# One product with v for both outer key blocks, kept zeros, DVE's other work behind the minimum, and both ends rearranged, in a hybrid attention layer

## The chip, the cores and the metric

The kernel runs on one core of a Trainium2 chip. TensorE (PE) multiplies matrices, VectorE (DVE) and ScalarE (ACT) work on tiles, GpSimd (POOL) does a few tile operations and issues some transfers, SyncE (SP) issues most transfers. The metric is device microseconds of one execution. A separate profiled execution gives the trace; its rows give start and length of each instruction in microseconds.

## The reference, cut to what matters

One layer of an encoder, 512 tokens, width 2048, all float32:

```
h = x @ w_in                                    # (512, 2048) x (2048, 8192)
qa, ka, va, ga, qb, kb, vb, gb = split(h, 1024 columns each)
ya = dilated_attention(qa, ka, va, t5 bias)     # 16 heads of 64, group A
yb = neighbourhood_attention(qb, kb, vb, rpb)   # 16 heads of 64, group B: 8 x 64 grid,
                                                # window of 8 rows x 16 columns
y = concat(ya * silu(ga), yb * silu(gb))
x = layer_norm(alpha * x + y @ w_out) * gain + bias
```

In group B a query sees keys of all 8 rows but of 16 columns only. The kernel cuts the 64 columns into four blocks of 16 queries; the two inner blocks meet 32 key columns each, the two outer ones (0 and 3) 24 each.

## The kernel before, in words

**Products.** Each float32 operand is split in two halves of a shorter format, a high one (ACT copies and rounds it) and a low one (DVE subtracts), by the helper `split` (lines 87 and 88). A product is then three products: high x high, high x low, low x high. Weights come as tiles of 128 x 1024, loaded by SP into a ring of raw tiles, split into a ring of six halves h0 to h5.

**Stages.** `plain_block` (from line 256) makes the gates of the first six head pairs, 16 steps of one tile of x and one of weights; its first weight and x tiles come in slices, so that PE can begin early, and nine products of a zero tile (`WARM`, line 123) run ahead of it. Six `strassen_block`s make k, q and v. From step 0 on, a hand-written order runs the attention: 128 pairs (head h, block b), n = 4h + b, each with `scores(n)`, a minimum over scores plus bias (`softmax`: L520 on DVE; biases have negative sign, so the minimum stands for the maximum), an exponent on ACT (L524), two steps later `turn` (transposes L578 on PE, high copy L583 on ACT, low half L584 on DVE), and in steps with n % 4 = 2 the product with v of the head before (`values`, L596), whose halves are added by L717 (ACT) and L718 (DVE). Between them `fill` puts products of later gates (L459) and of the first half of the output projection (L645). The scores and the product with v share two accumulator banks (`pss`).

**Order.** `later(k, fn)` hands work of ACT and DVE to the close of a step k steps on; `close()` runs it. So the low half of a weight tile (L445), the gate's second part (L465), yk's low half (L630) and copies of partial sums (L651) stand in DVE's order at the end of a step. PE, SP, DVE and ACT keep this written order in the attention; elsewhere a scheduler with a simulated timeline orders each engine, except DVE at the end.

**Group B.** A block's exponent is written to a tile p of two chunks of 128 key positions; the outer blocks fill 192 of 256 columns, and POOL sets the other 64 to zero each time (L567). `near` (line 586) lists the products with v: key chunk, query range, and place in the turned tile; chunk 3 is met by query blocks 0 and 3 in two products of 128 columns.

**End.** The second half of the output projection runs in two parts: column blocks 0 and 1 for all rows, then for each of four row tiles t the column blocks 2 and 3 with weights kept on chip (`wlast`). Then `residual`, `finish` (L765 sum, L766 statistics) and `norm(t)`: aggregate (L782), reciprocal square root (ACT L783, DVE L785), per column block a centring times the gain (L775) and a rescale plus bias (L779), and a transfer out.

Of the kernel before, what the change touches and what calls it, by code (L numbers as in the profile page):

```python
# [6 lines left out]
F32 = mybir.dt.float32  # L7
# [17 lines left out]
WARM = 9  # L25
# [45 lines left out]
def hybrid_layer(tc, xT, xn, w_in, w_early, w_gate, w_out, t5x, brow, rpb, cmask, eye, gain, lbias, out):  # L71
    nc = tc.nc
    from contextlib import ExitStack
    with ExitStack() as ctx:
# [181 lines left out]
        def plain_block(src):  # L256
# [15 lines left out]
            for i in range(8):  # L272
                xr = slot(f"r{i}", F32, "xraw")[:, :1024].rearrange("p (s q) -> p s q", s=2)
                raws.append(xr)
                for s in range(2):
                    k, n = i + 8 * s, 2 * i + s
                    if n == 0:
# [3 lines left out]
                        def xpart(c):  # L281
                            nc.sync.dma_start(xr[:, 0, c], xT[0][:, c])
                            split(xr[:, 0, c], X[0][:, 0, c], X[0][:, 1, c])

                        def wpart(c):
                            nc.sync.dma_start(raw[:, c], src[0][:, c])
                            split(raw[:, c], w[0][:, c], w[1][:, c])
# [142 lines left out]
        def later(k, fn):  # L430

            tasks.setdefault(step[0] + k, []).append(fn)

        def prepare():
# [10 lines left out]
            later(2, lambda: nc.vector.tensor_tensor(l, raw, f(h), ALU.subtract))  # L445
# [7 lines left out]
        def gate_unit(j):  # L453
# [15 lines left out]
            later(1, second)  # L469
# [39 lines left out]
        def softmax(sc, bias, n, grp, i, col, to=0):  # L509

            s = s_ring.next("s")
            p = p_ring.next("p")
# [22 lines left out]

        def load_bias(h):
            g, _, _, hg = head(h)
            bias = ring_b.next("bias")
            n = BW if g else 560
            nc.sync.dma_start(bias[:, :n], bias_d[g][hg])  # L540
            biases[h] = bias

        def scores(n):
# [14 lines left out]
            if g == 0:  # L558
# [3 lines left out]
            at = BIAS[(0, 1, 1, 2)[b]][0]  # L562
            p, exponent = softmax(sc, biases[h][:, at:at + 8 * w].rearrange(rows, r=8), 8 * w, 1, i, 4 * a + b,
                                  64 if b == 0 else 0)
            if w == 24:
                none = 0 if b == 0 else 192
                nc.gpsimd.memset(p[:, none:none + 64], 0.0)  # L567
# [18 lines left out]
        near = ((0, 0, 256, 128), (3, 0, 128, 0), (2, 256, 512, 640), (1, 128, 384, 384), (3, 384, 512, 896))  # L586
        full = tuple((k, 0, 512, 512 * k) for k in range(4))

        def values(h):
# [4 lines left out]
            for m, src in enumerate(turned.pop(h)):  # L594
                for n, (kc, q0, q1, at) in enumerate(parts):
                    nc.tensor.matmul(pv[:, q0:q1], vv[:, kc, a], src[:, at:at + q1 - q0],  # L596
                                     start=m == 0 and n == 0, stop=m == 1 and n == len(parts) - 1)
# [24 lines left out]
        def gated(i):  # L622
# [5 lines left out]
            later(0, lambda: nc.vector.tensor_tensor(y, y, rcs[i], ALU.mult))  # L628
# [275 lines left out]
```

## Time and profile before

| what | value |
| --- | --- |
| timed runs, median (lowest, highest) | 987.69 us (987.32, 988.73) |
| profiled execution, its own time | 987.23 us |
| its span, first to last instruction | 985.4 us |
| PE, DVE, ACT, POOL busy share | 99%, 77%, 50%, 21% |
| mean granted clock of PE | 0.996 |
| stages, by the trace | first products from 4.5 us, first block to about 75, k, q, v to about 560, attention to about 890, output to 975, last normalisation to 985 |

In a row, "x10" counts instructions merged in it, and a bracket tells how long the engine was idle before it and what ended that. A product's length contains its way through the array, so the steps from start to start give the pace.

### The profile page before, as it was taken

What the parts mean: (1) busy time and instruction counts of PE and PEld (TensorE: products, weight loads), DVE (VectorE), ACT (ScalarE), POOL (GpSimd) and SP (SyncE); (2) the same over time, 40 slices, a digit from 0 to 9 for tenths busy, and PEclk for the clock granted to TensorE, in tenths of its full rate; (3) what the DMA queues carried; (4) which work ended last, traced back from release to release, by engine and by line L of the source; (5) the groups of instructions that cost most, each with busy time, mean ns of one, the idle gap of its engine ahead of it and who ended that gap; (6) DMA issues with size and microseconds to landing.
All of it is one profiled execution on the core that took longest, in us unless ns stands there. A gap on an engine that the chain in (4) does not pass through costs nothing.

```text
span 985.4 us, 16207 instructions
## 1 busy us (share of the span) xinstructions
PE 971.5 (99%) x5883; PEld 858.3 (87%) x5883; DVE 756.0 (77%) x1146; ACT 491.6 (50%) x839; POOL 207.6 (21%) x354
## 2 busy tenths in 40 slices
PE   9999999999999999999999999999999999999995
PEld 7889999999888999999888888888888888888885
DVE  7958779678888887877988467676766867777877
ACT  7544444344444344434455365666666676763200
POOL 1003646754754620000000001101110011000021
PEclk9999999999999999999999999999999999999998
DMA  9823697698387558339435967777778788778222
GB/s 345 296 104 70 184 290 251 187 260 234 118 265 250 167 156 274 88 100 270 126 102 171 303 185 208 210 214 234 187 210 232 182 234 207 198 224 294 84 76 96
DMA packets 115888, 194.27 MB, mean 197 GB/s; under 512 B 46351, under 2 KB 65295, under 8 KB 115808
## 3 DMA queue, kind: packets, MB, share of 16 engines
q1 hardware_dynamic: 103552, 169.77, 57.0%
q0 software_dynamic: 12256, 23.47, 8.4%
q8 instruction: 46, 0.75, 0.3%
q14 instruction: 34, 0.28, 0.1%
HBM read 148.67 MB, written 44.50 MB: 196 GB/s over the span
## 4 chain that ended last, share of the span: by engine, by line
PE 95%; DVE 1%; ACT 1%; issue 1%; DMA 1%; POOL 0%; SPq 0%; ACTq 0%; POOLq 0%
PE acc L645 14%; PE acc L459 11%; PE acc L367 11%; PE acc L365 11%; PE acc L366 11%; PE acc L358 5%; PE acc L359 5%; PE acc L360 5%; PE pv L596 4%; PE pt L578 4%; PE acc L267 2%; PE acc L268 2%; PE acc L269 2%; PE sc L556 2%; PE sc L557 2%; PE sc L645 1%
## 5 line engine op out<-in xcount | busy, mean ns | idle before, releaser
L87 ACT ACTIVATE wh<-braw 128x1024 fp32r<-128x1024 f32 x168 | 178.2, 1061 | 239.8 <-PE acc L366 165.2
L88 DVE TENSOR_TENSOR wl<-braw,wh 128x1024 fp32r<-128x1024 f32 x168 | 206.2, 1229 | 74.7 <-ACT wh L87 74.6
L365 PE MATMUL acc<-xk,wh 128*128 128x256 f32 x512 | 143.6, 282 | 1.1 <-ACT wh L87 1.1
L366 PE MATMUL acc<-xk,wh 128*128 128x256 f32 x512 | 143.5, 282 | 0.0
L367 PE MATMUL acc<-xk,wl 128*128 128x256 f32 x512 | 141.1, 282 | 0.0
L373 DVE TENSOR_TENSOR braw<-braw 128x1024 f32<-128x1024 f32 x96 | 117.3, 1235 | 1.1
L645 PE MATMUL acc<-wh,yk 128*128 128x512 f32 x320 | 109.0, 403 | 0.0
L365 PE MATMUL acc<-op,wh 128*128 128x256 f32 x384 | 107.4, 282 | 0.0
L366 PE MATMUL acc<-op,wh 128*128 128x256 f32 x384 | 107.4, 282 | 0.0
L584 DVE TENSOR_TENSOR tl<-pt,th 128x256 fp32r<-128x256 f32 (+1 forms) x128 | 71.1, 555 | 44.8 <-ACT th L583 43.5
L367 PE MATMUL acc<-op,wl 128*128 128x256 f32 x384 | 105.2, 283 | 0.0
L524 ACT ACTIVATE p<-s,mn 128x512 f32<-128x512 f32 (+2 forms) x128 | 76.8, 600 | 51.1 <-DVE mn L520 50.6
L365 PEld LDWEIGHTS acc<-xk,wh 128*128 128x128 f32 x512 | 97.2, 190 | 1.6 <-ACT wh L87 1.5
L366 PEld LDWEIGHTS acc<-xk,wh 128*128 128x128 f32 x512 | 97.2, 190 | 0.1
L367 PEld LDWEIGHTS acc<-xk,wl 128*128 128x128 f32 x512 | 95.8, 190 | 0.0
L583 ACT ACTIVATE th<-pt 128x256 fp32r<-128x256 f32 (+1 forms) x128 | 62.4, 490 | 58.1 <-PE pt L578 55.9
L459 PE MATMUL acc<-xk,wh 128*128 128x512 f32 x320 | 91.0, 403 | 0.0
L520 DVE CUSTOM_DVE_ANT_0 s<-sc,bias 128x512 f32<-128x512 f32 (+2 forms) x128 | 68.0, 531 | 14.6 <-PE sc L557 14.2
L367 PEld LDWEIGHTS acc<-op,wl 128*128 128x128 f32 x384 | 71.5, 190 | 1.7 <-DVE wl L88 1.7
L365 PEld LDWEIGHTS acc<-op,wh 128*128 128x128 f32 x384 | 73.0, 190 | 0.0
L366 PEld LDWEIGHTS acc<-op,wh 128*128 128x128 f32 x384 | 73.0, 190 | 0.0
L645 PEld LDWEIGHTS acc<-wh,yk 128*128 128x128 f32 x320 | 58.5, 189 | 8.9
(157 smaller groups left out, 2036.1 us busy)
## 6 DMA issues: line engine op xcount, KB each, us to landing
braw<-in_w_in SPq DMA_DIRECT2D x96, 512.0 KB
wraw<-in_w_out SPq DMA_DIRECT2D x32, 512.0 KB
wraw<-in_w_gate SPq DMA_DIRECT2D x20, 512.0 KB
k_d<-kst SPq DMA_DIRECT2D x64, 128.0 KB
q_d<-kst SPq DMA_DIRECT2D x64, 128.0 KB
v_d<-vst SPq DMA_DIRECT2D x32, 256.0 KB
q<-q_d SPq DMA_DIRECT2D x32, 256.0 KB
k<-k_d SPq DMA_DIRECT2D x16, 512.0 KB
```

Of the source, the lines that this page charges most:

```text
L87: nc.scalar.activation(hi, raw, AF.Copy)
L88: nc.vector.tensor_tensor(lo, raw, f(hi), ALU.subtract)
L365: nc.tensor.matmul(o, h[:, c], ah, start=k == 0 and n == 0, stop=False)
L366: nc.tensor.matmul(o, h[:, c], al, start=False, stop=False)
L367: nc.tensor.matmul(o, l[:, c], ah, start=False, stop=k == 7 and n == 1)
L373: nc.vector.tensor_tensor(dst[u], dst[u], other[u], ALU.add)
L459: nc.tensor.matmul(acc, w[:, k * 128:k * 128 + 128], X[8 * u + k][:, s], start=u == 0 and n == 0 and k == 0, stop=u == 1 and n == 2 and k ...
L520: nc.vector.tensor_tensor_reduce(*flat, bias, 1.0, 3e38, ALU.add, ALU.min, mn)
L524: nc.scalar.activation(p[:, to:to + n].rearrange("p (b r c) -> p b r c", r=8, c=c), s[:, :n].rearrange(order, r=8, c=c), AF.Exp, bias=mn, ...
L583: nc.scalar.activation(th, pt[:, :nch], AF.Copy)
L584: nc.vector.tensor_tensor(tl, pt[:, :nch], f(th), ALU.subtract)
L645: nc.tensor.matmul(acc[:, part], yk[k][:, s, c], w[:, wk], start=first and kk == 0 and n == 0, stop=last and kk == 1 and n == 2)
```

## The change

It has five parts.

1. **Products with v, group B.** The two products of 128 columns with key chunk 3 become one of 256, which reads the first and the last 128 columns of the turned tile and writes query blocks 0 and 3 of the bank. The turned tile itself is as before.
2. **Kept zeros.** The two bias tiles b0 and b1 are taken once; columns 640 to 1151 of each hold the two outer blocks' p, whose 64 zero columns POOL sets once. The 32 memsets in the attention go.
3. **DVE's order.** `later` marks DVE work; work due at the close of a step n with n % 4 = 1 (5 to 127) is held and run in the next step behind its scores and minimum.
4. **The start.** x's first two slices are issued by ACT, the two slices of the first weight tile by SP in a row; DVE instead of ACT makes the first high half of x; six warm-up products instead of nine; ACT's first table load is for a copy.
5. **The end.** For the last row tile a function of its own: blocks 0 and 1 are multiplied by the gain ahead of time, their shift (bias minus mean x scale x gain) is made by PE from rows of gain and bias in high and low halves (`shift_rows`, with two loads and ten small transfers on SP ahead), and a single rescale follows. The transfers out alternate between SP and ACT, the last one in two halves.

The core of the diff, in the order of the file:

```diff
-WARM = 9
+WARM = 6
...
-                        wpart(slice(0, 256))
-                        xpart(slice(0, HALF))
-                        xpart(slice(HALF, S))
-                        wpart(slice(256, width))
+                        with tc.manual_schedule(engines={mybir.EngineType.Activation}):
+                            for c in (c0, c1):
+                                nc.scalar.dma_start(xr[:, 0, c], xT[0][:, c])
+                            nc.scalar.activation(warm, eps, AF.Copy)
+                        for c in (near, far):
                             nc.sync.dma_start(raw[:, c], src[0][:, c])
+                        nc.scalar.activation(w[0][:, near], raw[:, near], AF.Copy)
+                        nc.vector.tensor_copy(X[0][:, 0, c0], xr[:, 0, c0])
+                        nc.vector.tensor_tensor(X[0][:, 1, c0], xr[:, 0, c0], f(X[0][:, 0, c0]), ALU.subtract)
+                        nc.vector.tensor_tensor(w[1][:, near], raw[:, near], f(w[0][:, near]), ALU.subtract)
+                        split(xr[:, 0, c1], X[0][:, 0, c1], X[0][:, 1, c1])
+                        split(raw[:, far], w[0][:, far], w[1][:, far])
...
+        two, outers = [slot(f"b{i}", F32, "biases") for i in range(2)], []
+        for t in two:
+            outers.append((t[:, 640:896], t[:, 896:1152]))
+            nc.gpsimd.memset(t[:, 640:704], 0.0)
+            nc.gpsimd.memset(t[:, 1088:1152], 0.0)
...
+            outer = {0: (64, outers[h % 2][0]), 3: (0, outers[h % 2][1])}
             p, exponent = softmax(sc, biases[h][:, at:at + 8 * w].rearrange(rows, r=8), 8 * w, 1, i, 4 * a + b,
-                                  64 if b == 0 else 0)
-            if w == 24:
-                none = 0 if b == 0 else 192
-                nc.gpsimd.memset(p[:, none:none + 64], 0.0)
+                                  *outer.get(b, ()))
...
-        near = ((0, 0, 256, 128), (3, 0, 128, 0), (2, 256, 512, 640), (1, 128, 384, 384), (3, 384, 512, 896))
+        near = ((0, 0, 256, 128), (2, 256, 512, 640), (1, 128, 384, 384), (3, 0, 512, 0))
...
+                    o, w = pv[:, q0:q1], src[:, at:at + q1 - q0]
+                    if g and kc == 3:
+                        o = pv.rearrange("p (b q) -> p b q", b=4)[:, 0::3]
+                        w = src[:, 0:1024].rearrange("p (s q) -> p s q", s=8)[:, 0::7]
+                    nc.tensor.matmul(o, vv[:, kc, a], w, start=m == 0 and n == 0, stop=m == 1 and n == 3)
...
-            for fn in tasks.pop(step[0], ()):
-                fn()
+            for fn, dve in tasks.pop(step[0], ()):
+                if dve and 5 <= step[0] < 128 and step[0] % 4 == 1:
+                    held.append(fn)
+                else:
+                    fn()
...
                 exponent = scores(n) if n < 128 else None
+                while held:
+                    held.pop(0)()
...
+        def shift_rows():
+            raw, parts = slot("u0", F32, "lnraw"), slot("h0", F32R, "lnparts")
...
+            for r, at in enumerate((0, 16, 0, 8, 24)):
+                for c in range(2):
+                    nc.sync.dma_start(f(two[r:r + 1, c]), f(parts[:, at + 4 * c:at + 4 * c + 4]))
...
+            centre(3)
+            nc.vector.reciprocal(rs, rs)
+            nc.vector.scalar_tensor_tensor(nm, mv[:, 0:1], -1.0, rs, op0=ALU.mult, op1=ALU.mult)
+            nc.vector.tensor_copy(nms[:, 0:2], nm.to_broadcast([128, 2]))
+            nc.vector.tensor_tensor(nms[:, 2:3], nm, f(nms[:, 0:1]), ALU.subtract)
+            flat = bank(pst, "pt")[0:8, 0:128]
+            nc.tensor.transpose(flat, f(nms), ident)
...
+                nc.tensor.matmul(c, left[0:5], rows[0:5, i], start=True, stop=True)
...
+            rescale(3, whole, bb[3])
+            centre(2)
+            rescale(2, whole, bb[2])
+            rescale(0, whole, shifts[0])
+            for part in (slice(0, 256), slice(256, 512)):
+                rescale(1, part, shifts[1][:, part])
...
+                    if (t, dc) == (3, 2):
+                        for i in range(2):
+                            nc.vector.tensor_tensor(z[t][i], z[t][i], gb[i], ALU.mult)
```

How the order moves at the places that matter. First PE in one group-B step with a product with v (sc are scores, pv the product, th and tl the turned tile's halves, L459 and L464 filling products, pt transposes). Before:

```order
L557 MATMUL sc<-k,ql 128x256
L596 MATMUL pv<-th,vv 128x256
L596 MATMUL pv<-th,vv 128x128
L596 MATMUL pv<-th,vv 128x256 x2
L596 MATMUL pv<-tl,vv 128x256
L596 MATMUL pv<-tl,vv 128x128
L596 MATMUL pv<-tl,vv 128x256 x2
```

and now:

```order
L569 MATMUL sc<-k,ql 128x256
L610 MATMUL pv<-th,vv 128x256 x3
L610 MATMUL pv<-th,vv 128x2x128
L610 MATMUL pv<-tl,vv 128x256 x3
L610 MATMUL pv<-tl,vv 128x2x128
```

Ten products have become eight, the narrow ones gone (each 128-column row of before stands twice in its half; the second is left out above).

Second, DVE in a step with a product with v, near 848 us in the trace (mn is the minimum, yk a half of the gated output, z a partial sum, y the sum of the product's halves). Before:

```order
L584 TENSOR_TENSOR tl<-pt,th 128x256
L630 SCALAR_TENSOR_TENSOR yk<-y,yk 128x512
L651 COPY z_8847<-acc 128x512
L520 ISA s,mn<-sc,bias 128x512
L520 ISA mn 128x1
L718 TENSOR_TENSOR y<-pv,tmp 64x512
```

and now:

```order
L594 TENSOR_TENSOR tl<-pt,th 128x256
L525 ISA s,mn<-sc,biases 128x512
L525 ISA mn 128x1
L643 SCALAR_TENSOR_TENSOR yk<-y,yk 128x512
L664 COPY z_8759<-acc 128x512
L736 TENSOR_TENSOR y<-pv,tmp 64x512
```

The two other pieces of work now stand between the minimum and the sum y; 20 of the attention's steps have one or two such pieces.

Third, SP ahead of the last row tiles (lnrows are the rows of gain and bias, wraw the raw weight tiles):

```order
L897 DMA wraw<-in_w_out 128x1024 x2
L766 DMA gain<-in_lbias 128x512
L897 DMA wraw<-in_w_out 128x1024 x3
L825 DMA lnrows<-lnparts 1x128x4 x10
L897 DMA wraw<-in_w_out 128x1024
```

Ten small transfers stand ahead of the last weight tile, where before the last four weight tiles were issued in a row.

More of the change, by code (lines that the diff above doesn't have):

```diff
@@ L428, in hybrid_layer, with later @@
         step, tasks = [-PROLOGUE], {}
-        def later(k, fn):
-            tasks.setdefault(step[0] + k, []).append(fn)
+        held = []
+        def later(k, fn, dve=False):
+            tasks.setdefault(step[0] + k, []).append((fn, dve))
         def prepare():
@@ L468, in gate_unit @@
             later(0, lambda: nc.scalar.activation(sg, acc, AF.Tanh, scale=0.5))
-            later(1, second)
+            later(1, second, True)
         lows = []
@@ L665, in out_first @@
                     if u == 3:
[L666 removed]
+                        later(0, lambda t=t: keep(t, z[t][dc // 2][:, dc % 2], accs[t]), t % 2 == 1)
         def fillers():
@@ L732, in hybrid_layer @@
                 if n >= 8 and n % 8 == 4:
-                    later(0, lambda i=i: gate(i - 1))
+                    later(0, lambda i=i: gate(i - 1), True)
                 if n >= 8 and n % 8 == 7:
@@ L801, in norm @@
             nc.sync.dma_start(out[t * 128:t * 128 + 128, 0:512], zt)
+        def shift_rows():
+            raw, parts = slot("u0", F32, "lnraw"), slot("h0", F32R, "lnparts")
+            for i, src in enumerate((gain, lbias)):
+                nc.sync.dma_start(raw[:, 8 * i:8 * i + 8].rearrange("p (c j) -> p c j", c=2),
+                                  _view(src, 0, [[4, 128], [512, 2], [1, 4]]))
+            split(raw[:, :16], parts[:, :16], parts[:, 16:32])
+            two = slot("h1", F32R, "lnrows").rearrange("p (c q) -> p c q", c=2)
+            for r, at in enumerate((0, 16, 0, 8, 24)):
+                for c in range(2):
+                    nc.sync.dma_start(f(two[r:r + 1, c]), f(parts[:, at + 4 * c:at + 4 * c + 4]))
+            return two
@@ new lines, in last_norm, with centre, rescale @@
+        def last_norm(rows):
+            t = 3
+            mv = small.tile([128, 2], F32, name="mv", tag="mv")
+            rs = small.tile([128, 1], F32, name="rs", tag="rs")
+            nm = small.tile([128, 1], F32, name="nm", tag="nm")
+            nc.vector.bn_aggr(mv, st[t])
+            nc.scalar.activation(rs, mv[:, 1:2], AF.Sqrt, bias=eps)
+            def centre(i):
+                zt = z[t][i]
+                nc.vector.scalar_tensor_tensor(zt, zt, mv[:, 0:1], gb[i], op0=ALU.subtract, op1=ALU.mult)
+            queues = [nc.sync, nc.scalar]
+            def rescale(i, part, by):
+                zt = z[t][i][:, part]
+                nc.vector.scalar_tensor_tensor(zt, zt, rs, by, op0=ALU.mult, op1=ALU.add)
+                queue = queues.pop(0)
+                queues.append(queue)
+                queue.dma_start(out[384:512, 512 * i + part.start:512 * i + part.stop], zt)
+            whole = slice(0, 512)
+            centre(3)
[5 more added lines that the diff above has]
+            nc.tensor.transpose(flat, f(nms), ident)
+            shifts = []
+            left = slot("h3", F32R, "lnleft")[0:8, 0:128]
+            nc.scalar.activation(left, flat, AF.Copy)
+            for i in range(2):
+                c = bank(pacc, "acc")
+                nc.tensor.matmul(c, left[0:5], rows[0:5, i], start=True, stop=True)
+                shifts.append(c)
+            rescale(3, whole, bb[3])
[4 more added lines that the diff above has]
+                rescale(1, part, shifts[1][:, part])
@@ L819, in hybrid_layer @@
         load_x(1)
-        warm = small.tile([128, 1], F32, name="warm", bufs=1)
-        nc.scalar.activation(warm, eps, AF.Sqrt)
+        rows = shift_rows()
+        nms = small.tile([128, 8], F32R, name="nms", bufs=1)
+        nc.gpsimd.memset(f(nms), 1.0)
         wts = {}
@@ L842, in hybrid_layer @@
                         finish(dc, t, accs[m], part, dc + m)
-                    if dc == 3:
+                    if (t, dc) == (3, 2):
+                        for i in range(2):
+                            nc.vector.tensor_tensor(z[t][i], z[t][i], gb[i], ALU.mult)
+                    if dc == 3 and t < 3:
                         norm(t)
+                    elif dc == 3:
+                        last_norm(rows)
 def _weights(w_in, w_out):
```

30 lines of the change are left out of this document (9 added, 21 removed).

## The prediction

> **What bounds the kernel now.** I read the page first, then the waits of the matmul engine, then the windows by stage, and only then the places that the change touches. The first three rows below are from the page (span, busy shares, the chain of work that ended last), the fourth from the windows by stage.
>
> ```profile
> span 985.4 us, 16207 instructions
> PE 971.5 (99%) x5883; PEld 858.3 (87%) x5883; DVE 756.0 (77%) x1146; ACT 491.6 (50%) x839; POOL 207.6 (21%) x354
> PE 95%; DVE 1%; ACT 1%; issue 1%; DMA 1%; POOL 0%; SPq 0%; ACTq 0%; POOLq 0%
> 560.00:840.00 280.00, 279.67 (x1508) 232.89 (x1507) 193.14 (x449) 181.50 (x425) 30.26 (x76) 1.00 0.76 212
> ```
>
> PE is the bound from its first real product to its last, also in the attention stage (560 to 840 us), where DVE has 193 of 280 us of work. So a microsecond is won only where PE issues less, where PE stands still, or at the two ends where PE has nothing to do. The profiled execution took 987.23 us (985.4 of span and 1.8 around it); the median of the three timed runs is 987.69, 0.46 more. I work against the profiled one and add 0.46 at the end.
>
> **Part 1, one product for both outer key blocks.** Starts of PE rows in one group-B product with v (columns: start us, us, engine, line, operation), then 256-column products of the projection, then the 24 products of 128 columns at the very end:
>
> ```profile
> 595.73 0.39 PE L459 MATMUL acc<-xk,wh 128*128 128x512 f32 x1
> 595.96 0.28 PE L556 MATMUL sc<-k,q 128*128 128x256 f32 x1
> 596.20 0.68 PE L596 MATMUL pv<-th,vv 128*128 128x256 f32 x5
> 596.72 0.74 PE L596 MATMUL pv<-tl,vv 128*128 128x256 f32 x5
> 597.29 0.45 PE L459 MATMUL acc<-xk,wh 128*128 128x512 f32 x1
> 597.58 0.38 PE L578 MATMUL pt<-ident,p 128*128 128x128 f32 x2
> ...
> 99.80 0.28 PE L366 MATMUL acc<-xk,wh 128*128 128x256 f32 x1
> 101.92 0.28 PE L366 MATMUL acc<-xk,wh 128*128 128x256 f32 x1
> ...
> 972.26 2.79 PE L645 MATMUL sc<-wlast,yk 128*128 128x128 f32 x24
> ```
>
> The durations overlap, so I count from start to start. The ten products (six of 256 columns, four of 128) take 597.29 - 596.20 = 1.09 us, and the 512-column product behind them takes 0.29 instead of the 0.23 between 595.73 and 595.96: 1.15 us in all. Between 99.80 and 101.92 lie 18 steps of 256 columns, 0.118 us each. The 24 narrow products took 2.79 us, 0.116 each. So a 128-column product costs as much as one of 256: 6 x 0.118 + 4 x 0.116 = 1.17, near the 1.15 seen. The change makes eight of 256 columns: 8 x 0.118 = 0.94. That is 0.2 us less, and group B has 16 heads: **3.2 us**. The new product reads two runs of 128 columns and writes two runs; the rows at 100 us already read their moving operand in runs of 16 (the keys' reordering of line 365) and pay nothing for it. The strided write to the accumulator is in no row; bounds are 0 (it costs as much as the two it replaces) and 3.6 us; I take 3.2, since reads in runs are free.
>
> By the Trainium skill, "TensorE: Matmul & The Clock Gate", section "Back-to-back issue gap", an isolated warm product takes N/2.4 + 2.5 ns, so merging two of 128 into one of 256 would save 2.5 ns, and the 32 merged products 0.1 us together, an estimate; the same section gives 81 ns per product of 128 in a stream with weight loads. The trace has 116 ns and disagrees with the formula, so I go by the rows.
>
> **Part 2, kept zeros and DVE's order.** In a step with a product with v, PE's next scores need the accumulator bank whose minimum DVE has not yet taken. The fence shows the worst such place, then the sums of PE's weight-load waits.
>
> ```profile
> 847.39 0.40 PE L557 MATMUL sc<-k,ql 128*128 128x512 f32 x1
> 848.12 0.68 DVE L630 SCALAR_TENSOR_TENSOR yk<-y,yk 128x512 fp32r<-128x512 f32 x1
> 848.72 0.68 DVE L651 COPY z<-acc 128x512 f32<-128x512 f32 x1
> 849.32 0.68 DVE L520 CUSTOM_DVE_ANT_0 s<-sc,bias 128x512 f32<-128x512 f32 x1
> 850.07 0.19 PEld L556 LDWEIGHTS sc<-k,q 128*128 128x128 f32 x1 [0.64 <-DVE mn L520]
> 851.59 0.69 DVE L718 TENSOR_TENSOR y<-pv,tmp 64x512 f32<-64x512 f32 x1 [1.58 <-ACT tmp L717]
> ...
> PEld sc L556 <- DVE mn L520: 1.4, 4, 0.6
> PEld pt L578 <- POOL p L567: 0.5, 1, 0.5
> ```
>
> The scores were in the bank by 847.8, but DVE took the minimum (L520) only at 849.32, behind L630 and L651; PE waited 0.64 us. The change puts those two behind the minimum, which then starts 1.2 us earlier, more than the 0.6 that was lost. Such waits sum to 1.4 us in 4 places. The moved work lands in the idle 1.58 us ahead of L718, which waits for ACT, and ACT's wait shrinks too, because its exponent follows the minimum. What is late next is the weight's low half or yk, moved behind one minimum (0.68 us); both are used a whole weight tile or more later. If that cover were gone, each of 20 such steps could cost up to 0.6 us. The 32 memsets on POOL go; one held a transpose for 0.5 us. Of 1.4 + 0.5 = 1.9 us I take **1.6**, since PE arrives sooner by Part 1 and some waits return; bounds 0.5 and 2.1.
>
> **Part 3, the last row tile.** DVE rows of the end:
>
> ```profile
> 972.46 0.56 DVE L765 TENSOR_TENSOR z<-acc,z 128x384 f32<-128x384 f32 x1 [0.27 <-PE acc L645]
> 975.09 0.29 DVE L765 TENSOR_TENSOR z<-sc,z 128x128 f32<-128x128 f32 x1 [1.48 <-PE sc L645]
> 975.75 0.29 DVE L782 BATCH_NORM_AGGREGATE mv<-st 128x2 f32<-128x30 f32 x1
> 976.07 0.75 DVE L775 SCALAR_TENSOR_TENSOR z<-z,mv,gain 128x512 f32<-128x512 f32 x1
> 976.74 0.15 DVE L785 RECIPROCAL rs<-rs 128x1 f32<-128x1 f32 x1
> 976.93 0.75 DVE L779 SCALAR_TENSOR_TENSOR z<-z,rs,gain 128x512 f32<-128x512 f32 x1
> 981.28 0.75 DVE L779 SCALAR_TENSOR_TENSOR z<-z,rs,gain 128x512 f32<-128x512 f32 x1
> ```
>
> Before: eight wide operations from 976.07 to 982.03, 0.72 apart. Blocks 0 and 1 are now multiplied by the gain ahead of time: two operations of 0.6 in front of 972.46, filling 0.27 + 1.48 us of idle, hidden with 0.5 to spare; without that cover they would cost 1.2. Behind the aggregate stand two centrings, three rescales and one rescale in halves (0.43 each, by the 256-column row of DVE in Part 4): 6 x 0.72 + 0.15 for the split, plus three tiny operations at 0.19: 5.0 us against 5.96, so 0.95 less. PE's transpose and two small products, with ACT's copy between, take at most 0.38 + 0.63 + 2 x 0.40 = 1.8 us by rows quoted in Parts 1, 2 and 4, and have three wide DVE operations, 2.2 us, until the first rescale that reads them. The last transfer is 128 KB instead of 256 KB; at the 268 GB/s of the window in Part 4 half of it is 0.5 us, and I take half of that, 0.25, since several transfers end there together. Sum **1.2**, bounds 0.5 and 1.7.
>
> **Part 4, the start.** Rows of SP, of one window, of DVE, PE and ACT; the window row ends with the clock, the DMA share and the GB/s.
>
> ```profile
> 1.19 0.89 SPq L282 DMA_DIRECT2D xraw<-in_xT  x2
> 2.12 0.44 SPq L286 DMA_DIRECT2D wraw<-in_w_early  x1
> 2.50:3.00 0.50, 0.50 (x3) 0.15 (x1) 0.00 (x0) 0.09 (x1) 0.50 (x2) 1.00 0.92 268
> 4.32 0.43 DVE L324 TENSOR_TENSOR sums<-xraw 128x256 f32<-128x256 f32 x1
> 1.32 3.48 PE L124 MATMUL sc<-calm 128*128 128x512 bf16 x9 [1.32 <-POOL calm L121]
> 4.45 0.59 PE L267 MATMUL acc<-xk,wh 128*128 128x256 f32 x2
> 5.90 0.63 ACT L87 ACTIVATE wh<-wraw 128x512 fp32r<-128x512 f32 x1 [1.17 <-DMA wraw<-in_w_early]
> 6.59 0.50 PE L267 MATMUL acc<-xk,wh 128*128 128x512 f32 x1 [0.36 <-ACT wh L87]
> ```
>
> PE's steady stream begins at 6.59, and what ends last is the second weight slice, issued at 2.12 behind the first and two of x. It now takes the place that x had on SP at 1.19, while ACT issues x. The bytes that must land first are the same 640 KB, and the DMA engines are 0.92 busy already at 2.5 to 3 us, so the 0.9 us of earlier issue does not come through whole: **0.4**. ACT's first table load moves 0.9 us later, behind two issues of 0.44; I count nothing for it, since ACT waits for the first slices in any case. Against it: three warm-up products fewer. The nine took 0.39 us each on average, against 0.23 for a later one of 512 columns; six end at about 3.7, and the first real product can start little later. If PE is still slow then, its twelve 256-column products take up to 1.4 us more (0.118 each again), partly inside the wait for the slice. Bounds: -0.8 and 1.1.
>
> By the Trainium skill, "TensorE: Matmul & The Clock Gate", section "Part 1: The HAM clock gate", the clock doubles after about 3.4 us of sustained work, counted in time; by that rule six products (2.3 us by the row) and a gap would leave PE slow for the first real ones. The trace agrees that the early ones are slow (0.39 against 0.23); what the rule would cost is the lower bound just given.
>
> **Sum.** 3.2 + 1.6 + 1.2 + 0.4 = 6.4; 987.23 - 6.4 = 980.8 us, and with the 0.46 to the median **981.3 us**.
>
> **The rivals.**
>
> First, narrow products are cheap. If a 128-column product cost half of a 256-column one (0.059), ten would take 6 x 0.118 + 4 x 0.059 = 0.94, the same as eight, and Part 1 would give nothing: 984.5 us. For it: within the ten, each narrow one is short. Against it: the whole takes 1.15, not 0.94. The skill's formula named above would give this. A strided write at half rate ends near the same place. Chance 0.07.
>
> Second, the waits move instead of going: minima are early, but held work delays the sum L718 and so the bank for the scores after next. Part 2 gives nothing: 982.9. For it: one bank pair serves scores and products with v. Against it: 1.58 us of idle ahead of L718. Chance 0.14.
>
> Third, the slower side: the last weight tile queues on SP behind ten little transfers of the gain and bias rows.
>
> ```profile
> 909.94 13.18 SPq L827 DMA_DIRECT2D wraw<-in_w_out  x4
> 927.69 1.06 ACT L87 ACTIVATE wlast<-wraw 128x1024 fp32r<-128x1024 f32 x1 [5.30 <-DMA wraw<-in_w_out]
> 930.00 42.25 PE L645 MATMUL acc<-wlast,yk 128*128 128x512 f32 x191
> rc_d<-tmp POOLq DMA_DIRECT2D x16, 4.0 KB, 3.9
> ```
>
> The last tile was issued at 922.8 and split by 930. PE needs it for the last six of the first 48 products, 42 x 0.22 after 930: 939.3. So 9.3 us of delay are free. Issued at 0.4 each the ten cost 4 us, and the load still lands in time. If each waited for the one ahead, at the 3.9 us of the nearest small transfer, the delay would be 39 us and PE would lose 29.7: 981.3 + 29.7 = 1011 us. It costs from 9.3 us of delay on, and turns the whole slower from 9.3 + 6.4 = 15.7. Against it: SP issues other transfers without waiting. Chance 0.04.
>
> **How the numbers follow.** Forecast 0.75, rivals 0.07, 0.14 and 0.04. The forecast's own range, from its bounds, is 979.8 to 983; with the first two rivals the range is 979.7 to 984.6. A measurement of this kernel can tell 0.2%, about 2 us. All cases but the third rival lie 3 us or more below 987.69, so faster has 0.94; I leave 0.03 for no change, should two terms fail together, and 0.03 for slower.
>
> **What would show it.** In the changed trace: group-B products with v of 0.94 us from first start to the next product; no rows of PE's loads waiting on the minimum in steps with such a product; DVE ending 5 us after the last aggregate starts its centring; the first 512-column product before 6.3 us; the last weight split well ahead of its use. I am wrong if the merged product's spacing is above 0.13 us, or if PE's busy share falls anywhere in the last 60 us.

## Result: 0.9944 of the time before

The changed kernel takes 982.23 us (median; 981.59 to 984.53), the kernel before beside it 988.03 us (987.32 to 989.21). The ratio is 0.9944 with a 95% interval of 0.9931 to 0.9956: 5.8 us less, about what was forecast (981.3). The sum of the terms is nearly right; two terms in it are not.

The profiled execution took 981.69 us. The page of the changed kernel has these rows for its span, the busy shares and the chain of work that ended last:

```profile
span 979.9 us, 16071 instructions
PE 969.0 (99%) x5851; PEld 855.5 (87%) x5851; DVE 757.6 (77%) x1152; ACT 488.5 (50%) x839; POOL 202.9 (21%) x327
PE 97%; ACT 1%; DVE 1%; issue 0%; POOL 0%; DVEq 0%; ACTq 0%; POOLq 0%
```

PE still bounds the kernel, with 2.5 us less of its own work (969.0 instead of 971.5) and a larger part of the chain (97% instead of 95%): both less to issue and less standing still.

For the comparison of all runs I cut each trace at the same events: the first and the last start of a product with v (the attention), the start of the last row tile's aggregate, the end of DVE's last instruction, and the end of the span. All in us, from one profiled execution each.

| kernel | first product of the second tile | first product with v | attention | aggregate to DVE's end | DVE's end to span's end | span |
| --- | --- | --- | --- | --- | --- | --- |
| before | 9.44 | 575.18 | 314.58 | 6.29 | 3.41 | 985.44 |
| changed | 9.34 | 575.12 | 309.61 | 5.29 | 3.87 | 979.91 |
| changed, second trace | 9.71 | 575.66 | 309.73 | 5.30 | 3.88 | 980.57 |

Between the last product with v and the aggregate nothing moved (85.99 and 86.02 us). So the 5.53 us of span come from the attention (-4.97), DVE's end (-1.00), the start (-0.06), and 0.46 are lost again behind DVE.

The attention first. PE's starts at the same product with v as in the prediction, now in the changed kernel:

```profile
595.91 0.28 PE L568 MATMUL sc<-k,q 128*128 128x256 f32 x1
596.02 0.28 PE L569 MATMUL sc<-k,ql 128*128 128x256 f32 x1
596.14 0.64 PE L610 MATMUL pv<-th,vv 128*128 128x256 f32 x4
596.62 0.64 PE L610 MATMUL pv<-tl,vv 128*128 128x256 f32 x4
597.10 0.40 PE L464 MATMUL acc<-xk,wh 128*128 128x512 f32 x1
597.34 0.38 PE L588 MATMUL pt<-ident,biases 128*128 128x128 f32 x2
```

Eight products take 597.10 - 596.14 = 0.96 us and the 512-column one behind them its usual 0.24. Over the sixteen heads of group B the median of such a product with v, counted with what the product behind it loses, is 0.947 us; before it was 1.157.

PE's waits of the attention, in the view of weight-load waits (us in total, times, longest), were 1.4 us on the minimum and 0.5 us on POOL. Both rows are gone from the changed kernel's list, and among the attention's waits for another engine one row is new:

```profile
PEld pv L610 <- ACT th L593: 0.7, 2, 0.4
```

The product with v now waits twice for the high half of the turned probabilities. The second place is told by the timeline of DVE, ACT and PE's loads:

```profile
840.60 0.68 DVE L641 TENSOR_TENSOR y<-y,rc 128x512 f32<-128x512 f32 x1
841.20 0.68 DVE L525 CUSTOM_DVE_ANT_0 s<-sc,biases 128x512 f32<-128x512 f32 x1
841.92 0.72 ACT L529 ACTIVATE p<-s,mn 128x512 f32<-128x512 f32 x1 [1.39 <-DVE mn L525]
842.65 0.62 ACT L642 ACTIVATE yk<-y 128x512 fp32r<-128x512 f32 x1
843.17 0.57 ACT L666 ACTIVATE z<-acc 128x512 f32<-128x512 f32 x1
843.64 0.37 ACT L593 ACTIVATE th<-pt 128x256 fp32r<-128x256 f32 x1
844.06 0.42 PEld L610 LDWEIGHTS pv<-th,vv 128*128 128x128 f32 x3 [0.37 <-ACT th L593]
```

The minimum at 841.20 stands behind L641, which was closed in a step with n % 4 = 3 and is therefore not held. ACT idles 1.39 us for it, then does the exponent and two copies (L642, L666) before L593, for which PE stands still 0.37 us.

The last row tile, from the timeline of DVE and the queues:

```profile
970.75 0.29 DVE L834 BATCH_NORM_AGGREGATE mv<-st 128x2 f32<-128x30 f32 x1
971.07 0.75 DVE L839 SCALAR_TENSOR_TENSOR z<-z,mv,gain 128x512 f32<-128x512 f32 x1
972.41 0.74 DVE L845 SCALAR_TENSOR_TENSOR z<-z,rs,gain 128x512 f32<-128x512 f32 x1
973.28 1.21 PE L863 MATMUL acc<-lnrows,lnleft 5*128 5x512 f32 x2 [0.36 <-ACT lnleft L860]
974.52 1.53 DVE L845 SCALAR_TENSOR_TENSOR z<-z,rs,acc 128x512 f32<-128x512 f32 x3
974.63 1.40 ACTq L848 DMA_DIRECT2D out<-z  x2
975.29 1.12 SPq L848 DMA_DIRECT2D out<-z  x2
```

From the first centring (971.07) DVE needs 4.97 us to its end at 976.04, as worked out (5.0); PE's two shift products began at 973.28, 1.2 us ahead of the rescale that reads them. But the span ends 3.87 us behind DVE instead of 3.41.

### The profile page after: what moved, and what is told of

Its sections match the earlier page's. It is cut to its first block, busy times and chain, and to the rows that moved or that the text cites. A ratio compares the mean times of both kernels' runs of the same rounds, so it can differ in the third digit from the quotient of the medians.

```text
span 979.9 us, 16071 instructions
## 1 busy us (share of the span) xinstructions
PE 969.0 (99%) x5851; PEld 855.5 (87%) x5851; DVE 757.6 (77%) x1152; ACT 488.5 (50%) x839; POOL 202.9 (21%) x327
## 4 chain that ended last, share of the span: by engine, by line
PE 97%; ACT 1%; DVE 1%; issue 0%; POOL 0%; DVEq 0%; ACTq 0%; POOLq 0%
PE acc L658 14%; PE acc L464 11%; PE acc L369 11%; PE acc L367 11%; PE acc L368 11%; PE acc L360 5%; PE acc L361 5%; PE acc L362 5%; PE pv L610 4%; PE pt L588 4%; PE acc L267 2%; PE acc L268 2%; PE acc L269 2%; PE sc L569 2%; PE sc L568 2%; PE sc L658 1%
## 5 line engine op out<-in xcount | busy, mean ns | idle before, releaser
L593 ACT ACTIVATE th<-pt 128x256 fp32r<-128x256 f32 (+1 forms) x128 | 62.3, 489 | 64.8 <-PE pt L588 62.8
L464 PE MATMUL acc<-xk,wh 128*128 128x512 f32 x320 | 90.8, 402 | 0.0
L525 DVE CUSTOM_DVE_ANT_0 s<-sc,biases 128x512 f32<-128x512 f32 (+2 forms) x128 | 68.1, 532 | 17.9 <-PE sc L569 17.3
L529 ACT ACTIVATE p<-s,mn 128x512 f32<-128x512 f32 (+1 forms) x96 | 62.2, 647 | 25.8 <-DVE mn L525 25.5
```

The costliest lines, as they stand in the source:

```text
L464: nc.tensor.matmul(acc, w[:, k * 128:k * 128 + 128], X[8 * u + k][:, s], start=u == 0 and n == 0 and k == 0, stop=u == 1 and n == 2 and k ...
L525: nc.vector.tensor_tensor_reduce(*flat, bias, 1.0, 3e38, ALU.add, ALU.min, mn)
L529: nc.scalar.activation(p[:, to:to + n].rearrange("p (b r c) -> p b r c", r=8, c=c), s[:, :n].rearrange(order, r=8, c=c), AF.Exp, bias=mn, ...
L593: nc.scalar.activation(th, pt[:, :nch], AF.Copy)
```

## Experiments

Each is the changed kernel with one edit, unless it says otherwise. The first three ask what each part of the attention's gain is worth.

**Two narrow products again.** Kept zeros, DVE's order and both ends stay.

```diff
-        near = ((0, 0, 256, 128), (2, 256, 512, 640), (1, 128, 384, 384), (3, 0, 512, 0))
+        near = ((0, 0, 256, 128), (3, 0, 128, 0), (2, 256, 512, 640), (1, 128, 384, 384), (3, 384, 512, 896))
```

> The changed kernel with key chunk 3 again in two products of 128 columns; all else as changed. Theory (a narrow product is held up by its weight load and costs 0.11 us, as one of 256 columns does): each group-B product with v takes 0.22 us longer, 16 of them 3.6 us, so the profiled span grows from 979.9 to about 983.5 and the ratio to the kernel before goes from 0.994 to 0.998. Rival (a narrow product costs half of a wide one): the span grows by less than 0.3 us.

984.74 us, ratio 0.9965 (0.9952 to 0.9979). A product with v takes 1.158 us again instead of 0.947, and the attention 312.47 us: 2.86 longer than in the changed kernel. On PE alone the sixteen products differ by 16 x 0.21 = 3.4 us, near the 3.6 expected; but this kernel's list of waits has no row for the product with v waiting on ACT. That wait (0.7 us) comes with the merged product: PE arrives earlier at the place where ACT is late. The attention is still 2.11 us shorter than before, which is what zeros and order give without the merge.

**Nothing held.**

```diff
-                if dve and 5 <= step[0] < 128 and step[0] % 4 == 1:
+                if False and dve:
                     held.append(fn)
```

> The changed kernel with DVE's other work run at the close of its step again, the kept zeros left in. Theory (holding removed PE's waits for the minimum, and the waits for the turned tile's high half that the changed kernel shows are there with and without it): PE's weight loads wait again for the minimum in some four places, 1.4 us, and the span grows by 1.2 to 1.6 us. Rival (the waits only changed their name, since ACT is late by as much): waits for the minimum come back, those for the high half go, and the span grows by less than 0.6 us.

984.24 us, ratio 0.996 (0.9948 to 0.9973); the attention is 311.97 us, 2.36 longer, more than the 1.2 to 1.6 expected. This kernel's waits of PE's loads:

```profile
PEld sc L568 <- DVE mn L525: 1.9, 3, 0.8
PEld pv L610 <- ACT th L593: 0.7, 2, 0.4
```

The waits on the minimum are back, and larger than before the change (1.9 against 1.4 us): the merged product brings PE to them earlier. The kept zeros can't be the reason for the two that grew most (0.19 to 0.39 us near 650 us, 0.43 to 0.77 near 733): they lie ahead of POOL's only wait, which stood at 837 us. The wait for ACT is there with and without holding, so the holding didn't make it.

**POOL clears again.** The kept zeros alone undone.

```diff
-            outer = {0: (64, outers[h % 2][0]), 3: (0, outers[h % 2][1])}
...
-                                  *outer.get(b, ()))
+                                  64 if b == 0 else 0)
+            if w == 24:
+                none = 0 if b == 0 else 192
+                nc.gpsimd.memset(p[:, none:none + 64], 0.0)
```

> The kept zeros alone undone: the outer blocks' probabilities go to the ring again and POOL clears 64 columns of each. Theory: the zeros are worth the one wait of a transpose for POOL that the trace of before shows, 0.5 us or a little more, attention 309.9 to 310.3 us, ratio 0.0003 to 0.0007 above the changed kernel's. Rival: POOL clears in time once DVE's held work no longer delays the minimum; attention 309.6 us and an unchanged time.

982.32 us, ratio 0.9939 (0.9927 to 0.9952), beside 981.99 and 0.9936 of the changed kernel on the same chip; the attention is 310.19 us, 0.46 to 0.58 longer than in the two traces of the changed kernel, and the old wait is back:

```profile
PEld pt L590 <- POOL p L579: 0.6, 1, 0.6
```

The times alone could not carry this (0.33 us); the row and the stage do.

**Held at n % 4 = 3 too.** If the chain read from the timeline above is the cause of the new wait, the minimum must come ahead of L641 and L664.

```diff
-                if dve and 5 <= step[0] < 128 and step[0] % 4 == 1:
+                if dve and 5 <= step[0] < 128 and step[0] % 2 == 1:
```

> The changed kernel with DVE's other work held behind the minimum also from the close of steps n with n % 4 = 3. Theory (the two waits for the high half, 0.7 us, come from the chain minimum, exponent, ACT's later copies, high half, whose first minimum stands behind DVE work closed in such a step): these waits shrink by half or more and the attention, 309.6 us from the first to the last product with v, gets 0.3 to 0.7 us shorter. Rival (ACT's own copies ahead of the high half are what delays it): no change within 0.15 us.

The attention is 308.99 us, 0.62 less, and the row of the product with v waiting on ACT is gone: the chain is the cause. The time, 982.16 us, ratio 0.9943 (0.9927 to 0.9959), shows none of it: two of its four runs took 981.2 us, two 983.1 and 983.4, and the profiled one, which is of the long ones, reached its first product with v 2.3 us later (577.40). Rows of its start:

```profile
5.93 0.42 ACT L87 ACTIVATE xk<-xraw 128x256 fp32r<-128x256 f32 x1 [2.06 <-DMA xraw<-in_xT]
6.39 0.79 PE L267 MATMUL acc<-xk,wh 128*128 128x256 f32 x2 [0.73 <-ACT xk L87]
9.58 0.63 PE L267 MATMUL acc<-xk,wh 128*128 128x512 f32 x1
10.28 0.40 PE L267 MATMUL acc<-xk,wh 128*128 128x512 f32 x1
```

A slice landed late, PE stood still 0.73 us, and its products stayed slow (0.63 us in length instead of 0.40) until about 10 us; in the changed kernel's trace they are fast from 6.27. In this trace the record of the granted clock begins at full clock only at 10.07 us, in the changed kernel's at 6.21. The edit concerns steps of the attention alone; the combination at the end, with the same edit, began as usual.

The next three are about the end.

**The old end.** `norm(3)` as before, without shift rows, on one queue.

```diff
-                    if (t, dc) == (3, 2):
-                        for i in range(2):
-                            nc.vector.tensor_tensor(z[t][i], z[t][i], gb[i], ALU.mult)
-                    if dc == 3 and t < 3:
+                    if dc == 3:
                         norm(t)
-                    elif dc == 3:
-                        last_norm(rows)
```

> The changed kernel with the last row tile normalised as before, all its transfers on SP, and without the rows of gain and bias. Theory (DVE's part is 0.98 us shorter in the changed kernel, but 0.44 us goes to transfers that end later behind DVE): span 0.5 us longer than 979.9, with 5.96 us from the first centring to DVE's end and 3.4 us from there to the end of the span (changed: 4.98 and 3.85). Rival (the predicted 1.2 us is in it and was lost elsewhere): span 1.2 us longer.

982.66 us, ratio 0.9942 (0.993 to 0.9955). DVE needs 6.29 us from the aggregate and 3.44 lie behind it, 9.73 together against 9.16: the new end is worth 0.57 us, not 1.2. DVE's 1.00 us is as predicted; what lies behind DVE has the wrong sign.

**The last block whole**, and **one queue**, two edits apart.

```diff
-            for part in (slice(0, 256), slice(256, 512)):
+            for part in (whole,):
                 rescale(1, part, shifts[1][:, part])
```

> The changed kernel with the last rescale and its transfer whole (256 KB in rows of 2 KB) instead of in two halves (rows of 1 KB). Theory (halving won nothing: the 1 KB rows move at 260 KB a microsecond against 390, so the halves queue behind block 0): from the last centring's start to DVE's end 5.17 us (changed 5.29), from there to the end of the span 3.4 to 3.7 (changed 3.87), span 0.2 to 0.5 us shorter. Rival (the smaller last transfer does save 0.25 us, as predicted, and something else cost 0.7): span 0.15 us or more longer.

```diff
-            queues = [nc.sync, nc.scalar]
+            queues = [nc.sync]
```

> The changed kernel with all transfers out of the last row tile on SP, halves kept. Theory (the transfers are held by the DMA engines and by how they are confirmed, not by the queue that issues them): 3.87 us behind DVE's end within 0.2. Rival (it is the second queue that delays the last one, since ACT's half and SP's half share the engines): 0.3 us or more shorter. Second rival (two queues helped): 0.3 us or more longer.

Whole: 981.51 us, ratio 0.9936 (0.992 to 0.9952), DVE's end 5.17 and 3.37 behind it. One queue: 981.94 us, ratio 0.9943 (0.9927 to 0.9958), 5.30 and 3.85. So the halving loses 0.5 us behind DVE and 0.12 on it, and the second queue does nothing. What the halves meet is seen in the transfer view, where each number is the GB/s of a quarter of a microsecond from 976 us on: the kernel before, then the changed one, then the one with the last block whole.

```profile
GB/s 0 0 0 0 0 0 0 0 0 0 303 393 336 17 0 16 377 385 271 0 0 66 385 393 205 0 0 172 377 385 115 0 0 0 0 0 0 0 0 0
```

```profile
GB/s 385 369 410 328 344 348 213 12 0 0 0 0 0 0 0 0 0 0 0 0 0 0 0 0 0 0 0 0 0 0 0 0 0 0 0 0 0 0 0 0
```

```profile
GB/s 369 385 377 393 369 377 393 369 58 0 0 0 0 0 0 0 0 0 0 0 0 0 0 0 0 0 0 0 0 0 0 0 0 0 0 0 0 0 0 0
```

Before, each of the four blocks (256 KB) travelled alone, in about 0.8 us with a gap to the next. Now three rescales follow one another with no centring between (973.85 to 976.04), the transfers have no gap, and the last bytes queue behind block 0: half a block less in the last transfer does not bring the last byte forward. The halves, with rows half as long, also go at 328 to 348 where whole blocks go at 369 to 410. But this explains little of the 0.5 us: the last byte arrives 1.85 us behind DVE's end with halves (up to 1.95 in the other traces that have them), 1.80 with the last block whole, and 1.69 before.

The rest lies in how SP closes the program. It goes through a list of waits for semaphores (counters by which transfers and engines report that they are done), and the trace records each wait. Where nothing is missing, the waits pass 0.06 us apart. SP's waits for transfers out of z, in us in total, times, longest: the kernel before, the changed one, the one with the last block whole.

```profile
SPq L899 <- DMA out<-z: 1.6, 2, 1.4
SPq L974 <- DMA out<-z: 2.0, 1, 2.0
SPq L974 <- DMA out<-z: 2.3, 3, 0.9
```

The last transfer's wait has a different place in the list in each, by these records and the time at which the transfer reports its landing (us):

| kernel | its place in the list | DVE's end until it passes | until the list is done | from there to the span's end | together |
| --- | --- | --- | --- | --- | --- |
| before | sixth, four follow | 2.28 | 0.31 | 0.82 | 3.41 |
| changed | third, seven follow | 2.55 | 0.50 | 0.82 | 3.87 |
| last block whole | last | 2.47 | 0.06 | 0.84 | 3.37 |

So of the 0.50 us between halves and the whole block 0.44 are the waits that follow in the list, and of the 0.46 us lost against before 0.27 are the later landing and 0.19 the list. No run moved these waits alone, so this is read from the records and not shown by an edit. The two values do return: 3.85 to 3.93 us behind DVE's end in the ten traces with halves, 3.37 and 3.41 in the two with the new end and a whole last block.

The last three are about the start.

**The old start** and **nine warm-ups.** The first restores the order of loads, the nine warm-up products and the early table load for the square root ahead of the last part; the second restores the nine alone.

```diff
-WARM = 6
+WARM = 9
```

> The changed kernel with the start of the kernel before (all four slices on SP, x copied by ACT, nine warm-up products, first table load as before). Theory (the second tile of x and w ends the start, and it lands when the bytes ahead of it have passed, whoever issues them): first product of the second tile within 0.15 us of the changed kernel's 9.34, span within 0.3 us of 979.9. Rival (the new start is worth the 0.4 us that the prediction gave it): span 0.4 us longer.

> The changed kernel with nine warm-up products instead of six. Theory (with six, the clock stays slow through the first twelve real products: they stand 0.21 us apart in the changed kernel, 0.12 in the kernel before; but the second tile's landing ends the start in any case): the first real products 0.12 us apart, first 512-column product 0.2 to 0.4 us earlier than the 6.6 of the changed kernel, first product of the second tile unchanged within the 0.25 us by which it varies from run to run (9.3 to 9.8 so far), span unchanged. Rival (the missing warm-up costs what the new start won): span 0.4 us or more shorter.

Old start: 982.55 us, ratio 0.9943 (0.9931 to 0.9956), first product of the second tile at 9.77 us, first product with v at 575.58. Nine warm-ups: 982.24 us, ratio 0.9943 (0.9926 to 0.9961), 9.92 and 575.61. The new start gave 9.04 to 9.87 in the other traces (without the 11.67 above). The expectations miss (9.77 instead of within 0.15 of 9.34; with nine warm-ups the first real products 0.21 us apart instead of 0.12), but the changed kernel's own second trace has 9.71, and neither edit stands out of that scatter. That the number of warm-ups decides is refuted by the trace with nine of them:

```profile
1.33 4.02 PE L124 MATMUL sc<-calm 128*128 128x512 bf16 x9 [1.33 <-POOL calm L121]
6.00 0.62 PE L269 MATMUL acc<-xk,wl 128*128 128x256 f32 x2
6.70 0.28 PE L268 MATMUL acc<-xk,wh 128*128 128x256 f32 x1
```

Here the same nine products took 4.02 us, not 3.48 as before, and real products stayed 0.21 apart until 6.4 us.

**POOL's loads later.** Three loads by POOL (198 KB, not read before 82 us) wait until the fourth tile is split.

```diff
+            nc.gpsimd.tensor_copy(ident[:, 0:1], f(X[9][:, 0, 0:1]))
             nc.gpsimd.dma_start(ident, eye)
...
+            nc.gpsimd.tensor_copy(bt[0:33, 0:1], f(X[9][0:33, 0, 0:1]))
+            nc.gpsimd.tensor_copy(t5[:, 0:1], f(X[9][0:33, 0, 0:1]))
             nc.gpsimd.dma_start(bt[0:33, :ROW], brow)
             nc.gpsimd.dma_start(t5, t5x)
```

> POOL's first three loads (ident 64 KB, brow 132 KB, t5x 2 KB) wait for the fourth tile's split, so they no longer travel with the first four tiles; nothing reads them before 82 us. Theory: what bounds the start is the bytes that must land ahead of the second tile's activations, some 1.5 MB with these 200 KB; without them it lands about an eighth of 5 us earlier, the first product of the second tile at 8.5 to 9.0 us, and the time 0.3 to 0.8 us below the changed kernel's. Rival: the start is set by the latency of the second tile's own transfer; then the product stays in 9.0 to 9.9 us and the time is unchanged.

981.85 us, ratio 0.9933 (0.9921 to 0.9946), beside 981.99 of the changed kernel: no difference that can be told. Yet the second tile of x is split earlier. First the changed kernel, then this one:

```profile
7.35 0.63 ACT L87 ACTIVATE xk<-xraw 128x512 fp32r<-128x512 f32 x1 [1.42 <-DMA xraw<-in_xT]
```

```profile
6.25 0.63 ACT L87 ACTIVATE xk<-xraw 128x512 fp32r<-128x512 f32 x1 [0.64 <-DMA xraw<-in_xT]
9.06 0.39 PE L270 MATMUL acc<-xk,wh 128*128 128x512 f32 x1
```

It landed 1.1 us earlier than in the changed kernel's trace. In the other traces with the new start the same split begins between 6.59 and 7.98 us, so a single trace 0.34 us ahead of all of them speaks for bytes and against latency, but doesn't show it. Its first product came at 9.06, only 0.28 earlier, and that isn't owed to the landing: in both traces PE goes from the first tile's products to the second's without a wait. The first tile's 512-column products began earlier by as much (6.32 instead of 6.61), and the record of full clock begins at 5.80 us instead of 6.21. The gain in time that the theory expected did not come.

**The changed kernel again**, the control for **POOL clears again**, **POOL's loads later** and the next, and **both mends together** (held at odd steps, last block whole):

> The changed kernel as it is, beside the next three on the same chip: ratio 0.994 again, attention 309.6 us, DVE's end 5.29 us, 3.9 us behind it; the first product of the second tile anywhere between 9.0 and 9.9 us, as in the nine profiles so far that show it there.

> DVE's later work is held behind the minimum in the steps with n % 4 == 3 too, and the last rescale with its transfer is one whole block. Theory: the two gains seen apart add, attention 309.0 us instead of 309.6, DVE's end 5.17 instead of 5.29 and 3.4 us behind it instead of 3.9, together 1.2 us, so the ratio is 0.0012 below that of the changed kernel in this call. Rival: the second hold is paid for at the start, whose first product of the second tile came at 11.67 us in its profile instead of 9.0 to 9.9; then it comes near 11.7 again and only the 0.6 us of the end are left at most.

The changed kernel: 981.99 us, ratio 0.9936 (0.9923 to 0.9948). With both mends: 980.71 us (980.33 to 981.16), ratio 0.9922 (0.9909 to 0.9936). The five runs of each don't overlap (the control's lowest is 981.74), and the difference of 1.28 us is the 1.2 expected: attention 309.09, DVE's end 5.17, 3.41 behind it. Its start is ordinary (9.87 us), so the late one above belonged to those executions. This is the fastest version tried, 7.3 us below the kernel before.

## Why the prediction was right, and where it was not

| term | predicted, us | measured, us | by |
| --- | --- | --- | --- |
| Part 1, merged product | 3.2 | 3.4 on PE, 2.9 in the attention | sixteen products with v; undone alone |
| Part 2, zeros and order | 1.6 | 2.1 without the merge | narrow products against before |
| both together | 4.8 | 5.0 | attention before and after |
| Part 3, DVE | 0.95 | 1.00 | aggregate to DVE's end |
| Part 3, last transfer | 0.25 | -0.46 | DVE's end to the span's end |
| Part 4, start | 0.4 | about 0.1, not resolved | first product with v |
| sum | 6.4 | 5.5 | spans |

**Part 1 was right, in size and reason.** Eight products at the pace of 256 columns were put at 0.94 us and take 0.95; the strided write costs nothing that shows. This refutes the first rival. By the formula for an isolated product in the Trainium skill, "TensorE: Matmul & The Clock Gate", section "Back-to-back issue gap", 0.1 us would have been saved in all; the trace disagrees, with 0.21 in each of the sixteen. The section says itself that this formula counts too little for small products with weight loads between them. One reading of the prediction was slightly off: the 24 narrow products of the end stand 0.111 us apart from start to start in the trace of before, not 0.116, which was their whole length divided by 24. With 0.111 the ten products come to the 1.15 us that were seen. The two signs of being wrong stayed away: 0.947 us are 0.118 a product, and in the last 60 us PE is busy for 51.75 us, against 49.65 before.

**Part 2 was right in mechanism and mis-sized.** I added the waits in the trace of before, 1.4 + 0.5, and took a little off because PE would arrive sooner. Arriving sooner does the opposite: the waits grow, to 1.9 us on the minimum, when the merge is there and nothing is held. So holding is worth 2.4 us and the zeros 0.5 beside the merge. Undoing each of the three parts costs 2.86 + 2.36 + 0.58 = 5.8 us, 0.8 more than they give together. They guard one another, and here a term read from the trace of before was the lower end for a wait that a faster engine meets. The second rival (held work delays the sum) did not happen. A new wait did appear, of 0.7 us, but in ACT's line and behind work that was not held; the prediction looked for what is late next only behind the steps that it moved.

**Part 3's DVE term was right, its transfer term has the wrong sign.** The step that failed is "the last transfer is 128 KB instead of 256 KB; ... and I take half of that". I doubted it for the right reason (several transfers end together) but kept its sign. A DVE that finishes three blocks one behind the other makes the transfer engines, not DVE, decide when the last byte arrives: 256 KB in about 0.8 us each, against 0.66 us of DVE per block. From there on half a block less at the end did not make the last byte earlier (1.85 us behind DVE's end instead of 1.69). The other thing that the term left out is what SP does after the landing: the last half's wait stands early in SP's closing list, which costs 0.19 us against before. With the last block whole 0.50 us are back, 0.44 of them from that list.

**Part 4 was about nothing, inside its bounds.** The second weight slice is split at 5.31 instead of 5.90 us, as argued, but this is not what ends last any more. The predicted sign, a 512-column product before 6.3 us, failed (6.61; in the second trace of the changed kernel it came at 6.27). Rows of the changed kernel:

```profile
5.05 0.63 PE L269 MATMUL acc<-xk,wl 128*128 128x256 f32 x2
5.31 0.62 ACT L87 ACTIVATE wh<-wraw 128x512 fp32r<-128x512 f32 x1
6.38 0.28 PE L268 MATMUL acc<-xk,wh 128*128 128x256 f32 x1
6.61 0.40 PE L267 MATMUL acc<-xk,wh 128*128 128x512 f32 x1
```

The bound of 1.4 us for slow products was named and left out of the likeliest value; a good part of it came. I blamed it on fewer warm-ups, and that reason fell: in the two later traces with nine, full clock came as late (6.13 and 6.48 us). The trace's record of the granted clock, which the lengths of the products bear out (0.41 us for 256 columns ahead of it, down to 0.28 behind), begins at full clock at 4.12 us before, at 6.21 in the changed kernel, at 4.14 to 6.91 in eleven other traces, and at 10.07 in one. The Trainium skill, "TensorE: Matmul & The Clock Gate", section "Part 1: The HAM clock gate", says so beside the rule that I quoted: the activity window runs freely, so that the number of slow products varies from run to run for the same kernel. The traces agree (4.12 to 10.07 us), and a term of 0.4 us that rests on the first 6 us of one profiled execution can't be told from it. The slow products are not the whole story either: four traces of the new start had full clock by 5.1 us, and their second tile began at 9.60 to 9.79 us, later than in five of the other eight with the new start. In two of these four PE waited 0.5 us there for the second tile of weights; in the changed kernel's own trace it didn't wait. What ends the start differs between executions and stays open.

**The third rival** was priced right as harmless. The ten small transfers and the last weight tile in the changed kernel:

```profile
914.35 7.77 SPq L825 DMA_DIRECT2D lnrows<-lnparts  x10
SPq L825 <- DVE lnparts L88: 1.5, 1, 1.5
922.16 0.59 SPq L897 DMA_DIRECT2D wraw<-in_w_out  x1
925.86 1.06 ACT L87 ACTIVATE wlast<-wraw 128x1024 fp32r<-128x1024 f32 x1 [6.44 <-DMA wraw<-in_w_out]
```

SP issues them in 7.8 us: about 0.64 from one to the next instead of the 0.4 taken, with one wait of 1.5 us in between for DVE's low halves of the rows, and not the 3.9 of the rival. Counted from the last product with v the tile is split 3.2 us later than before (41.1 against 37.9), within the free 9.3; no wait of PE belongs to it.

The total is 0.9 us above the forecast (981.69 against 980.8 in the profiled execution, 982.23 against 981.3 in the median): 0.7 too much was expected of the end and 0.3 of the start, 0.2 too little of the attention. The range given with the forecast, 979.8 to 983, is narrower than the bounds of its four terms, which add up to 979.2 to 987.5; the prediction doesn't say how it was narrowed, so that the measured time lies inside it says less than it seems.

## What to carry to other kernels

Read the price of a small product from start-to-start steps of its kind in the trace; here 128 columns cost what 256 do, and merging them pays by the count. When an engine is made faster, its waits elsewhere can grow (here from 1.4 to 1.9 us): follow each chain that ends in a wait back through all engines, and ask again behind every step that was not moved. At the end of a program, compare the pace of the producer with that of the transfers before cutting the last piece smaller: here a shorter last transfer queued behind the others and landed no earlier. Whether it helps where it travels alone was not tried. Look also at what follows the landing, down to the order of the closing waits.

## What was not expected of the hardware

- The moment at which PE gets its full clock differs between executions of nearly the same start, from 4.1 to 6.9 us and once 10.07 by the trace's record. In that one PE had also stood still for 0.73 us in the first 6.4 us, and the second tile began at 11.67 us instead of 9.0 to 9.9. Two other traces with such a wait (0.48 and 0.57 us) and full clock by 5.0 us began it at 9.79 and 9.75.
- While half blocks travelled the transfer engines moved 328 to 348 GB/s, with whole ones 369 to 410. The span ended 0.5 us later behind DVE with halves than with the last block whole, on one queue as on two, and in the traces shown only 0.05 us of that is the last byte; 0.44 are waits that SP still goes through after the landing, 0.06 us each.
- Small transfers from tile to tile left SP 0.64 us apart, where 0.4 had been taken from its loads at the start.
